# A two-layer decoder trunk: the residual stream turned from features on partitions to tokens on partitions

## The chip, the cores and the metric

One core of one Trainium2 chip runs the whole program. The metric is the device time of one execution in microseconds (us); the kernel before takes 875.04 us, the median of 3 runs (874.21 to 877.12).

## The reference

For each of two layers, on 256 tokens of 1024 features in float32 (cut to what matters):

```python
h = rmsnorm(x, norm_mix[i]);  z = h @ w_in[i]            # 1024 -> 5400 columns
y_a = nsa_mixer(...) @ w_up_nsa[i];  y_b = retention(...) @ w_up_ret[i]
mix = sigmoid(merge_a) * y_a + sigmoid(merge_b) * y_b
x = x + mix @ w_out[i]                                   # "out"
h = rmsnorm(x, norm_mlp[i])
x = x + square(relu(h @ w_ff1[i])) @ w_ff2[i]            # "ff1", "ff2": 1024 -> 4096 -> 1024
gate = sigmoid(rmsnorm(x, norm_ple[i]) @ w_ple_gate[i])  # "gate"
x = x + gate * (p[i] @ w_ple[i])                         # "ple"
```

`rmsnorm(x, g)` is x times the root r of 1/(mean of x squared + 1e-6), per token, times a gain per feature.

## The kernel before, in words

Every product is made of three TensorE matmuls in a 32-bit format of less precision: each operand is split in a high part (ScalarE copies it, `act`) and a low part (VectorE subtracts, `sub`), and `three` adds high x high, high x low and low x high in PSUM. The weights come from memory in units of 128 x 1024 floats (512 KB). For each unit SyncE issues a load into one of 4 `raw` buffers (line 310), ScalarE writes `hi` and VectorE writes `lo` (`unit_split`, lines 314 to 325), 6 buffers each, up to 4 units ahead of the one in use (`advance`, `take`). `PLAN` is the order of the units; the TensorE order is written out by hand (`ORDER`, and the body of `layer`), while the order of ScalarE, VectorE and GpSimd is left to the framework, which goes by readiness and priority. Generators for the attention work are put between the matmuls by a model of time (`poke`, `charge`).

The residual stream lies in `XT`, a tile of 128 x 8 x 256: feature within its chunk of 128 on the partitions, chunk, token. A norm stage (`new_stage`) holds `XH` and `XL`, the high and low parts of x times the gain, in the same layout; there are three stages in a layer (mixer, MLP, gate), and the factor r is brought in after the product. `feed_x` makes one chunk of `XH` (ScalarE, 256 columns) and of `XL` (VectorE, 256 columns). `feed_sq` squares two chunks (ScalarE) and adds the squares up, on VectorE or, for chunks 2 to 5, on GpSimd (`gp`, line 209). `finish_a` sums the squares over the partitions with matmuls against a column of ones (4 TensorE instructions `pt<-ones,z`) and makes r by a power on GpSimd; `finish_b` spreads r over the partitions with two TensorE transposes (`pt<-cst,r`, line 220) and a ScalarE copy to `RB`.

Two ways of multiplying stand in the kernel. In `b_unit`, `wide` and the loops of ple and gate the 128 x 128 weight block is stationary and 256 tokens stream past it: 24 matmuls of 256 columns for a unit. In `a_unit` (used for q, rv, rg and others of the first product) 128 x 128 of the activations are stationary and 512 weight columns stream: 12 matmuls of 512 columns for a unit.

The tail of a layer runs thus. `out` has 8 units; four accumulators, one for each two chunks of features, two in the PSUM tag `sc` and two in `pt`, take `wide` products (`out_k`). The last two units are used together for one accumulator after the other, and behind each accumulator VectorE adds it to `XT` and `feed` makes the stage of the MLP. `ff1` (16 pairs of units, PSUM tag `mm`) and `ff2` (32 units, the same four accumulators) then take turns. At the end of ff2 each accumulator is multiplied by `RB` (`dz`), added to `XT` and fed. `ple` has 2 units; its result `pw` waits in SBUF. `gate` has 8 units in four groups of two chunks; `gate_tail` multiplies by `RB`, takes tanh, multiplies with `pw`, adds to `XT`, and feeds the next layer's stage or, in the last layer, sends the chunks out. The next layer starts with the units kcvc, kvg and q, all from the fed stage.

Of the kernel before, what the change touches and what calls it, by code (L numbers as in the profile page):

```python
# [15 lines left out]
P = 128  # L16
# [29 lines left out]
for _n, _w in PAR_PARTS:  # L46
# [8 lines left out]

ORDER = (
# [7 lines left out]
def _seq(s):  # L64
    return [(x, 0) if x in ("fa", "fb") else (x[:-1], int(x[-1])) for x in s.split()]
# [5 lines left out]
def _plan(l):  # L71
    r = [({"w": "w1"}.get(n, n), u) for n, u in SEQ[l] if n not in ("fa", "fb")]
# [10 lines left out]
    r += [("gate", u) for u in (0, 2, 4, 1, 3, 5, 6, 7)]  # L83
    return [(l,) + x for x in r]
# [11 lines left out]
def trunk(ctx: ExitStack, tc: tile.TileContext, xT, wu, wg, cst, msk, par, pin, out):  # L96
# [131 lines left out]

    XT = bp.tile([P, 8, S], F32, tag="S0", name="XT")
    PR = [cp.tile([P, NHEAD], F32, tag=f"par{l}", name=f"par{l}") for l in range(DEPTH)]  # L230
# [44 lines left out]
    def load_early(k):  # L275
# [113 lines left out]
    def new_stage(l, which):  # L389
# [7 lines left out]
            "sq": None,  # L397
        }

    def feed_x(st, c0, n):  # L400
        t0 = cur[0]
        for c in range(c0, c0 + n):
            fresh(t0)
            g = st["g"][:, c:c + 1]
            act(st["XH"][:, c, :], XT[:, c, :], AF.Copy, scale=g)
            stt(out=st["XL"][:, c, :], in0=XT[:, c, :], scalar=g,
# [19 lines left out]
    def feed(st, c0, n=2):  # L426
        feed_x(st, c0, n)
        feed_sq(st, c0, n)

    def finish_a(st):  # L430
        sq = st["sq"]
        pr = p_tile([P, 2])
        for t in range(2):
            mm(pr[:, t:t + 1], sq[:, 0, t * P:(t + 1) * P], ones, start=True, stop=True)
        ms = small([P, 2], "ms")
        ts(out=ms, in0=pr, scalar1=1.0 / D, scalar2=EPS, op0=ALU.mult, op1=ALU.add)
# [4 lines left out]
    def finish_b(st, square=False):  # L441
# [5 lines left out]
        if square:  # L447
            act(RB, pb.rearrange("p a b -> p (a b)"), AF.Square)
        else:
            act(RB, pb.rearrange("p a b -> p (a b)"), AF.Copy)  # L450
# [43 lines left out]
    def layer(l, st):  # L494
# [392 lines left out]
        for name, u in SEQ[l]:  # L887
            if name == "kcvc":
                b_unit(pkv, take(l, "kcvc", u), XH, XL, 4 * u, u == 0, u == 1)
                if u == 1:  # L890
                    ready("kcvc")
            elif name == "fa":
# [98 lines left out]
        def accumulators():  # L991
            return [(s_tile, p_tile)[n % 2]([P, 2, S]) for n in range(4)]

        po = []

        def out_k(k):
# [3 lines left out]
            for n in range(4):  # L1000
                wide(po[n], w, n, MH[:, k, :], ML[:, k, :], k == 0, False)
# [21 lines left out]
        for n in range(4):  # L1023
            wide(po[n], w6, n, MH[:, 6, :], ML[:, 6, :], False, False)
            wide(po[n], w7, n, MH[:, 7, :], ML[:, 7, :], False, True)
            xc = XT[:, 2 * n:2 * n + 2, :]
            tt(out=xc, in0=xc, in1=po[n], op=ALU.add)
            feed(stf, 2 * n)
# [14 lines left out]
        def ff1(i):  # L1043
            pm = mm_tile([P, 2, S])
            for u in range(2):
                b_unit(pm, take(l, "ff1", 2 * i + u), XH, XL, 4 * u, u == 0, u == 1)
# [12 lines left out]
        def ff2(i):  # L1059
            h, o = ff.pop(i)  # L1060
            for u in range(2):
# [3 lines left out]
                for n in range(4):  # L1065
                    wide(pf[n], w, n, h[:, u, :], o[:, u, :], i == 0 and u == 0, False)

        ff1(0)
        finish_a(stf)
        ff1(1)  # L1070
        finish_b(stf, square=True)
        for i in range(14):
            ff1(i + 2)
# [4 lines left out]
        dz = [big([P, 2, 2, S], f"B{1 + i}", "dz") for i in range(2)]  # L1078
        h, o = ff.pop(15)
        for n in range(4):  # L1080
            for u in range(2):
                wide(pf[n], ws[u], n, h[:, u, :], o[:, u, :], False, u == 1)
            d = dz[n // 2][:, n % 2]
            tt(out=d, in0=pf[n], in1=bc2(stf["RB"]), op=ALU.mult)
            xc = XT[:, 2 * n:2 * n + 2, :]
            tt(out=xc, in0=xc, in1=d, op=ALU.add)
            feed(stp, 2 * n)


        pw = big([P, 8, S], "S5", "pw")  # L1090
        for u in range(2):
            wh, wl = take(l, "ple", u)
            vh = wh.rearrange("p (k n) -> p k n", k=2)
            vl = wl.rearrange("p (k n) -> p k n", k=2)
            for n in range(2):
                pm = mm_tile([P, 2, S])
                for k in range(2):
                    for q in range(2):
                        c = (2 * n + q) * P
                        three(pm[:, q, :], vh[:, k, c:c + P], vl[:, k, c:c + P], ph[:, k, :],  # L1100
                              pl[:, k, :], k == 0 and q == 0, k == 1 and q == 1)
                c = 4 * u + 2 * n
                with tc.high_priority():
                    act(pw[:, c:c + 2, :], pm, AF.Copy, scale=0.5)
# [4 lines left out]
        Z = [big([P, 4, S], f"B{3 * i}", "gz") for i in range(2)]  # L1109

        def gate_tail(pm, c0, n):
            z = Z[c0 // 4][:, c0 % 4:c0 % 4 + n, :]
            tt(out=z, in0=pm, in1=stp["RB"].unsqueeze(1).to_broadcast([P, n, S]), op=ALU.mult)
            act(z, z, AF.Tanh, scale=0.5)
            stt(out=z, in0=z, scalar=1.0, in1=pw[:, c0:c0 + n, :], op0=ALU.add, op1=ALU.mult)
            xc = XT[:, c0:c0 + n, :]
            tt(out=xc, in0=xc, in1=z, op=ALU.add)
            if stn is not None:
                feed(stn, c0, n)
            else:  # L1120
                nc.sync.dma_start(out[:, c0:c0 + n, :], xc)

        pms = [mm_tile([P, 2, S]) for _ in range(3)]
        for u in range(2):
            for j in range(3):
                b_unit(pms[j], take(l, "gate", 2 * j + u), XH, XL, 4 * u, u == 0, u == 1)
                if u == 1 and j == 0:
                    finish_a(stp)
                if u == 1 and j == 1:
                    finish_b(stp)  # L1130
                    gate_tail(pms[0], 0, 2)
                    gate_tail(pms[1], 2, 2)
        gate_tail(pms[2], 4, 2)
        ws = [take(l, "gate", 6 + u) for u in range(2)]
        for n in range(2):
            pm = s_tile([P, 1, S])
            for u in range(2):
                vh = ws[u][0].rearrange("p (k n) -> p k n", k=4)
# [143 lines left out]
```

## Time and profile before

| | |
|---|---|
| median of 3 runs | 875.04 us (874.21 to 877.12) |
| profiled execution | 876.97 us, of which the span from first to last instruction is 875.1 us |
| TensorE busy | 851.6 us, 97% of the span, 6649 matmuls |
| VectorE busy | 613.2 us (70%) |
| ScalarE busy | 502.6 us (57%) |
| GpSimd busy | 59.1 us (7%) |
| DMA | 152.11 MB, 174 GB/s on average |
| mean granted TensorE clock | 0.989 of full speed |

The busy time of TensorE counts a matmul from its start to its modelled end, which overlaps the next matmul; so how fast matmuls follow one another is read from their starts, or from the chain of work that ended last, which counts each piece only up to the next. In the profile, L215 is the matmul helper, L220 the transpose helper, L184 a ScalarE activation, L188 a VectorE two-tensor operation, L196 a VectorE scalar-tensor-tensor operation and L209 a GpSimd two-tensor operation. A tile is named with its operands, as `mm<-XH,hi`: written to `mm` from the moving `XH` and the stationary `hi`.

### The profile page before, as it was taken

To read this page: it belongs to the slowest core of one execution; us is meant where nothing else is said; L and a number is where in the kernel's file an instruction comes from. 1 tells how busy PE (TensorE), PEld (TensorE's weight loads), DVE (VectorE), ACT (ScalarE), POOL (GpSimd) and SP (SyncE) were. 2 spreads that over 40 slices of the span, in tenths; PEclk is the share of its full clock that TensorE was granted. 3 is DMA by queue.
4 is the path that set the end of the run, shared out by engine and by line. 5 is a ranking of instruction groups with operands and counts; after the bars stand their busy time and mean duration, and the time that the engine had idled before them with its cause. 6 is when DMAs were issued, how large, how long until landed. Compare 5 with 4: busy or idle time off the path is not lost.

```text
span 875.1 us, 16496 instructions
## 1 busy us (share of the span) xinstructions
PE 851.6 (97%) x6649; PEld 822.9 (94%) x6649; DVE 613.2 (70%) x997; ACT 502.6 (57%) x838; POOL 59.1 (7%) x44
## 2 busy tenths in 40 slices
PE   7989999989999999999999999999899999999997
PEld 6888899989999999999987988999899999999997
DVE  5988797866865555556898888887668555555585
ACT  6776786544654444445676878775347444444461
POOL 2120000000200000000222100000003000000020
PEclk8999999989999999999999999999999999999999
DMA  7857544436476656656655563543455666656541
GB/s 232 315 185 231 167 126 140 127 104 191 127 235 185 181 189 188 179 189 203 220 160 169 183 205 118 169 125 119 147 181 170 194 187 189 178 189 189 179 139 49
DMA packets 43852, 152.11 MB, mean 174 GB/s; under 512 B 5120, under 2 KB 6144, under 8 KB 43776
## 3 DMA queue, kind: packets, MB, share of 16 engines
q1 hardware_dynamic: 43776, 151.06, 55.8%
q8 instruction: 52, 0.85, 0.4%
q14 instruction: 24, 0.20, 0.1%
HBM read 149.99 MB, written 1.05 MB: 173 GB/s over the span
## 4 chain that ended last, share of the span: by engine, by line
PE 85%; DVE 8%; issue 2%; POOL 2%; DMA 1%; ACT 1%; SPq 0%; DVEq 0%; ACTq 0%; POOLq 0%
PE mm L215 51%; PE sc L215 16%; PE pt L215 14%; PE ot L215 3%; DVE lo L188 3%; PE pt L220 2%; POOL rso L209 1%; DMA raw<-in_wu_dram 1%; DVE zt L188 1%; DVE XL L196 1%; DVE zs L188 0%; ACT tmp L184 0%; DVE gz L196 0%; DVE XT L188 0%; ACT hi L184 0%
## 5 line engine op out<-in xcount | busy, mean ns | idle before, releaser
L188 DVE TENSOR_TENSOR lo<-raw,hi 128x1024 fp32r<-128x1024 f32 (+2 forms) x285 | 341.1, 1204 | 184.4 <-ACT hi L184 183.5
L184 ACT ACTIVATE hi<-raw 128x1024 fp32r<-128x1024 f32 (+2 forms) x285 | 295.5, 1045 | 280.1 <-PE mm L215 156.6
L215 PE MATMUL mm<-XH,hi 128*128 128x256 f32 x992 | 283.4, 286 | 0.0
L215 PE MATMUL mm<-XH,lo 128*128 128x256 f32 x992 | 279.3, 282 | 0.0
L215 PE MATMUL mm<-XL,hi 128*128 128x256 f32 x992 | 279.1, 281 | 0.0
L215 PEld LDWEIGHTS mm<-XH,hi 128*128 128x128 f32 x992 | 186.8, 188 | 1.1
L215 PEld LDWEIGHTS mm<-XL,hi 128*128 128x128 f32 x992 | 186.9, 188 | 0.8
L215 PEld LDWEIGHTS mm<-XH,lo 128*128 128x128 f32 x992 | 186.8, 188 | 0.0
L215 PE MATMUL pt<-ho,hi 128*128 128x256 f32 x512 | 96.6, 281 | 0.0
L215 PE MATMUL sc<-ho,hi 128*128 128x256 f32 x512 | 96.6, 281 | 0.0
L215 PEld LDWEIGHTS pt<-ho,hi 128*128 128x128 f32 x512 | 78.6, 188 | 0.0
L215 PEld LDWEIGHTS sc<-ho,hi 128*128 128x128 f32 x512 | 78.5, 188 | 0.0
L215 PE MATMUL sc<-ho,lo 128*128 128x256 f32 x256 | 72.0, 281 | 0.0
L215 PE MATMUL pt<-ho,lo 128*128 128x256 f32 x256 | 72.0, 281 | 0.0
L215 PE MATMUL mm<-hi,XH 128*128 128x512 f32 (+2 forms) x160 | 57.6, 360 | 0.0
L215 PE MATMUL mm<-hi,XL 128*128 128x512 f32 (+2 forms) x160 | 56.4, 352 | 0.0
L215 PE MATMUL mm<-lo,XH 128*128 128x512 f32 (+2 forms) x160 | 56.3, 352 | 0.0
L215 PEld LDWEIGHTS sc<-ho,lo 128*128 128x128 f32 x256 | 48.2, 188 | 0.0
L215 PEld LDWEIGHTS pt<-ho,lo 128*128 128x128 f32 x256 | 48.2, 188 | 0.0
L184 ACT ACTIVATE e<-e,nmx 128x128 f32<-128x128 f32 (+2 forms) x96 | 37.7, 395 | 11.9 <-DVE nmx L204 11.8
L209 POOL TENSOR_TENSOR rso<-rsv,mhalf 128x2 f32<-128x2 f32 (+3 forms) x18 | 23.8, 1324 | 295.8 <-DVE rsv L192 287.1
L209 POOL TENSOR_TENSOR z<-z,z 128x512 f32<-128x512 f32 x12 | 20.3, 1692 | 296.9 <-ACT pw L184 173.5
(181 smaller groups left out, 1345.0 us busy)
## 6 DMA issues: line engine op xcount, KB each, us to landing
raw<-in_wu_dram SPq DMA_DIRECT2D x275, 512.0 KB, 3.7
raw<-in_wg_dram SPq DMA_DIRECT2D x8, 280.0 KB, 3.2
XT<-in_xT_dram SPq DMA_DIRECT2D x3, 256.0 KB, 6.9
cst<-in_cst_dram SPq DMA_DIRECT2D x1, 768.0 KB, 7.9
out_dram<-XT SPq DMA_DIRECT2D x3, 256.0 KB, 2.4
raw<-in_wu_dram SPq DMA_DIRECT2D x2, 256.0 KB, 3.9
tmp<-in_pin_dram SPq DMA_DIRECT2D x2, 256.0 KB, 4.1
cmp<-in_par_dram SPq DMA_DIRECT2D x2, 144.0 KB, 4.4
```

What stands on the lines that cost most here:

```text
L184: return nc.scalar.activation(o, *a, **k)
L188: return nc.vector.tensor_tensor(**k)
L196: return nc.vector.scalar_tensor_tensor(**k)
L209: return nc.gpsimd.tensor_tensor(**k)
L215: return nc.tensor.matmul(o, a, b_, **k)
L220: return nc.tensor.transpose(o, a, i)
```

## The change

The stream is kept as `X`, 128 tokens on the partitions x 2 token halves x 1024 features. It is loaded from a second copy of the input (`xk`, 1 MB, issued on SyncE's queue behind the 40th weight unit) into the SBUF place of `XT`, which is only used for the first stage. In out, ff2, ple and gate the activations are now stationary and 512 weight columns stream (`wide`, `a_unit`); the four accumulators are quarters (token half, feature half) in the order (0,0), (1,0), (0,1), (1,1). With tokens on the partitions r is a factor per partition: ff2 adds its result with r squared in one VectorE operation, gate takes r in the scale of tanh, and `dz`, `RB` and `finish_b` go from those two stages. The squares are summed along the row by ScalarE (`square`, with an accumulator), so that `finish_a` needs no matmul and no GpSimd addition. For the stage of the next product `turn_x` turns half of the features: 8 TensorE transposes of 128 x 128 into two PSUM tiles, from which ScalarE and VectorE make `XH` and `XL`. The first half is turned behind the third quarter, the second half behind the first unit that uses the first half (at ff1, whose first four units are reordered), between the two ple units, or at `tr` in the next layer's order. The first layer's first stage is fed as before.

```diff
+    "kcvc0 kvg0 tr kvg1 kcvc1 fa kvg2 kvg3 fb q0 q1 q2 q3 w0 w1 ksvs0 ksvs1 w2 w3 w4 rq0 rq1 w5  "
...
-    r += [("ff1", u) for u in range(4)]
+    r += [("ff1", u) for u in (0, 2, 1, 3)]
...
+        if k == 40:
+            X.append(bp.tile([P, 2, D], F32, tag="S0", name="X"))
+            nc.sync.dma_start(X[0], xk)
...
+    def turn_x(st, n, tiles):
+        for j in range(2):
+            c0 = 4 * n + 2 * j
+            pt = tiles[j]([P, 2, S])
+            for c in range(2):
+                for t in range(2):
+                    flip(pt[:, c, t * P:(t + 1) * P], X[0][:, t, (c0 + c) * P:(c0 + c + 1) * P], ident)
+            feed_x(st, c0, pt)
+
+    def square(st, t, n):
+        if st["ss"] is None:
+            st["ss"] = small([P, 2, 2], "ssx")
+        act(ztile([P, 512]), xs(t, n), AF.Square, accum_out=st["ss"][:, t, n:n + 1])
...
-    def wide(o, w, n, ah, al, f, z):
-        for q in range(2):
-            c = (2 * n + q) * P
-            three(o[:, q, :], w[0][:, c:c + P], w[1][:, c:c + P], ah, al,
-                  f and q == 0, z and q == 1)
+    def wide(o, w, t, n, ah, al, f, z):
+        a, b = t * P, n * 512
+        three(o, ah[:, a:a + P], al[:, a:a + P], w[0][:, b:b + 512], w[1][:, b:b + 512], f, z)
...
+        for i, (t, n) in enumerate(quads):
+            wide(po[i], w6, t, n, MH[:, 6, :], ML[:, 6, :], False, False)
+            wide(po[i], w7, t, n, MH[:, 7, :], ML[:, 7, :], False, True)
+            fresh()
+            tt(out=xs(t, n), in0=xs(t, n), in1=po[i], op=ALU.add)
+            if i == 2:
+                turn_x(stf, 0, (mm_tile, mm_tile))
...
+        ff1_unit(0, 0)
+        turn_x(stf, 1, (s_tile, p_tile))
+        ff1_unit(1, 0)
+        for t, n in quads:
+            square(stf, t, n)
+        ff1_unit(0, 1)
+        ff1_unit(1, 1)
         finish_a(stf)
-        ff1(1)
-        finish_b(stf, square=True)
+        r2 = small([P, 2], "r2")
+        tt(out=r2, in0=stf["r"], in1=stf["r"], op=ALU.mult)
...
+            stt(out=xs(t, n), in0=pf[i], scalar=r2[:, t:t + 1], in1=xs(t, n), op0=ALU.mult, op1=ALU.add)
+            if i == 2:
+                turn_x(stp, 0, (mm_tile, mm_tile))
...
+        for n in range(2):
+            w = take(l, "ple", n)
+            pms = [mm_tile([P, 512]) for _ in range(2)]
+            a_unit(pms, w, ph, pl, 0, 2, 512, True, True)
...
+            if n == 0:
+                turn_x(stp, 1, (s_tile, p_tile))
+                for t, m in quads:
+                    square(stp, t, m)
+                finish_a(stp)
...
+        def gate_tail(pm, t, n):
+            fresh()
+            z = Z[n][:, t, :]
+            act(z, pm, AF.Tanh, scale=rg[:, t:t + 1])
+            stt(out=z, in0=z, scalar=1.0, in1=pw[:, t, n * 512:(n + 1) * 512], op0=ALU.add, op1=ALU.mult)
+            tt(out=xs(t, n), in0=xs(t, n), in1=z, op=ALU.add)
+            if stn is not None:
+                square(stn, t, n)
+            else:
+                nc.sync.dma_start(out[:, t, n * 512:(n + 1) * 512], xs(t, n))
...
+            if n == 1 and stn is not None:
+                turn_x(stn, 0, (s_tile, s_tile))
+            ws = [take(l, "gate", 4 * n + u) for u in (2, 3)]
+            for t in range(2):
...
+                gate_tail(pms[t], t, n)
```

## Rows read from the trace of the kernel before

**Rows 1.** The page: span, and busy time by engine (share, instructions).
```profile
span 875.1 us, 16496 instructions
PE 851.6 (97%) x6649; PEld 822.9 (94%) x6649; DVE 613.2 (70%) x997; ACT 502.6 (57%) x838; POOL 59.1 (7%) x44
```
**Rows 2.** The page: the chain that ended last, share by engine.
```profile
PE 85%; DVE 8%; issue 2%; POOL 2%; DMA 1%; ACT 1%; SPq 0%; DVEq 0%; ACTq 0%; POOLq 0%
```
**Rows 3.** The chain in time, first ff1 units: start us, us, what.
```profile
230.41 5.69 PE mm L215 x48
236.10 0.44 PE pt L215 x4
236.54 5.80 PE mm L215 x48
242.34 0.34 PE pt L220 x2
```
**Rows 4.** The 512-column matmuls: their group by form, then the chain.
```profile
L215 PE MATMUL mm<-lo,XH 128*128 128x512 f32 x96 | 37.8, 394 | 0.0
...
88.40 4.20 PE mm L215 x18
...
522.73 4.18 PE mm L215 x18
```
**Rows 5.** The chain, transposes between attention matmuls in layer 1.
```profile
544.68 0.44 PE pt L220 x4
545.12 0.71 PE mm L215 x6
```
**Rows 6.** The chain, gate of layer 1 to the end.
```profile
858.56 0.34 PE pt L215 x4
...
861.86 0.22 PE pt L220 x2
...
864.93 5.71 PE sc L215 x48
...
872.03 0.42 DVE XT L188
```
**Rows 7.** TensorE's timeline, start of layer 1; in brackets idle before, and releaser.
```profile
445.75 0.39 PE L215 MATMUL ot<-XL,hi 128*128 128x256 f32 x1 [0.46 <-DVE XL L196]
...
452.88 0.58 PE L215 MATMUL pt<-ones,z 128*128 128x1 f32 x4 [0.33 <-DVE z L188]
...
456.89 0.43 PE L220 MATMUL pt<-cst,r 128*128 128x128 f32 x2 [0.25 <-POOL r L209]
```
**Rows 8.** Stretches: length, busy PE, PEld, DVE, ACT, POOL; clock, DMA share, GB/s.
```profile
246.00:407.00 161.00, 161.00 (x1360) 161.00 (x1359) 88.37 (x87) 75.58 (x85) 0.95 (x1) 1.00 0.62 188
443.00:490.00 47.00, 43.27 (x286) 38.48 (x285) 41.55 (x75) 33.91 (x59) 13.64 (x9) 1.00 0.54 168
616.90:620.30 3.40, 3.40 (x16) 3.40 (x17) 0.98 (x1) 0.00 (x0) 0.00 (x0) 0.50 0.37 82
```
**Rows 9.** Timelines of VectorE, ScalarE and GpSimd: start us, us, operation.
```profile
408.88 1.23 DVE L188 TENSOR_TENSOR lo<-raw,hi 128x1024 fp32r<-128x1024 f32 x1 [1.62 <-ACT hi L184]
442.75 3.74 DVE L196 SCALAR_TENSOR_TENSOR XL<-XT,par,XH 128x256 fp32r<-128x256 f32 x4
471.99 0.88 DVE L196 SCALAR_TENSOR_TENSOR KT<-pt,gk,KT 128x256 fp32r<-128x256 f32 x2
...
407.79 1.06 ACT L184 ACTIVATE hi<-raw 128x1024 fp32r<-128x1024 f32 x1 [1.79 <-PE pt L215]
471.03 0.47 ACT L184 ACTIVATE KT<-pt,gk 128x256 fp32r<-128x256 f32 x1
...
442.70 2.71 POOL L209 TENSOR_TENSOR z<-z,z 128x512 f32<-128x512 f32 x2 [10.73 <-ACT z L184]
```
**Rows 10.** DMA issues of the result: KB each, median us to landing.
```profile
out_dram<-XT SPq DMA_DIRECT2D x3, 256.0 KB, 2.4
out_dram<-XT SPq DMA_DIRECT2D x2, 128.0 KB, 1.8
```

More of the change, by code (lines that the diff above doesn't have):

```diff
@@ L64, in _seq @@
 def _seq(s):
-    return [(x, 0) if x in ("fa", "fb") else (x[:-1], int(x[-1])) for x in s.split()]
+    return [(x, 0) if x in ("fa", "fb", "tr") else (x[:-1], int(x[-1])) for x in s.split()]
 SEQ = [_seq(s) for s in ORDER]
 def _plan(l):
-    r = [({"w": "w1"}.get(n, n), u) for n, u in SEQ[l] if n not in ("fa", "fb")]
+    r = [({"w": "w1"}.get(n, n), u) for n, u in SEQ[l] if n not in ("fa", "fb", "tr")]
     for n in ("ma", "mb"):
@@ L82, in _plan @@
     r += [("ple", u) for u in range(2)]
-    r += [("gate", u) for u in (0, 2, 4, 1, 3, 5, 6, 7)]
+    r += [("gate", u) for u in range(8)]
     return [(l,) + x for x in r]
@@ L424, in feed_sq, with xs @@
             tt(out=acc[:, 0], in0=acc[:, 0], in1=acc[:, 1], op=ALU.add)
-    def feed(st, c0, n=2):
-        feed_x(st, c0, n)
-        feed_sq(st, c0, n)
+    def xs(t, n):
+        return X[0][:, t, n * 512:(n + 1) * 512]
+    def turn_x(st, n, tiles):
[10 more added lines that the diff above has]
+        act(ztile([P, 512]), xs(t, n), AF.Square, accum_out=st["ss"][:, t, n:n + 1])
     def finish_a(st):
[L431 to L434, printed above, removed]
         ms = small([P, 2], "ms")
+        if st["ss"] is None:
+            pr = p_tile([P, 2])
+            for t in range(2):
+                mm(pr[:, t:t + 1], st["sq"][:, 0, t * P:(t + 1) * P], ones, start=True, stop=True)
+        else:
+            pr = small([P, 2], "ssum")
+            tt(out=pr, in0=st["ss"][:, :, 0], in1=st["ss"][:, :, 1], op=ALU.add)
         ts(out=ms, in0=pr, scalar1=1.0 / D, scalar2=EPS, op0=ALU.mult, op1=ALU.add)
@@ L439, in finish_a, with finish_b @@
         st["r"] = r
-    def finish_b(st, square=False):
+    def finish_b(st):
         r = st["r"]
@@ L891, in layer @@
                     ready("kcvc")
+            elif name == "tr":
+                turn_x(st, 1, (p_tile, p_tile))
             elif name == "fa":
@@ L1041, in layer, with ff1_unit, ff1_end @@
         sub(pl, pT, ph.bitcast(F32))
[L1043 to L1046, printed above, removed]
+        def ff1_unit(i, u):
+            if u == 0:
+                ff[i] = mm_tile([P, 2, S])
+            b_unit(ff[i], take(l, "ff1", 2 * i + u), XH, XL, 4 * u, u == 0, u == 1)
+            if u == 1:
+                ff1_end(i, ff[i])
+        def ff1_end(i, pm):
+            fresh()
             au = big([P, 2, 2, S], f"B{i % 3}", "au")
@@ L1077, in layer @@
         ws = [take(l, "ff2", 30 + u) for u in range(2)]
-        dz = [big([P, 2, 2, S], f"B{1 + i}", "dz") for i in range(2)]
         h, o = ff.pop(15)
-        for n in range(4):
+        for i, (t, n) in enumerate(quads):
             for u in range(2):
[L1082 to L1087, printed above, removed]
@@ L1090, in layer @@
[L1090 to L1104, printed above, removed]
+                wide(pf[i], ws[u], t, n, h[:, u, :], o[:, u, :], False, u == 1)
@@ new lines, in layer @@
+            fresh()
+            stt(out=xs(t, n), in0=pf[i], scalar=r2[:, t:t + 1], in1=xs(t, n), op0=ALU.mult, op1=ALU.add)
+            if i == 2:
+                turn_x(stp, 0, (mm_tile, mm_tile))
+        pw = big([P, 2, D], "S5", "pw")
+        for n in range(2):
+            w = take(l, "ple", n)
+            pms = [mm_tile([P, 512]) for _ in range(2)]
+            a_unit(pms, w, ph, pl, 0, 2, 512, True, True)
+            with tc.high_priority():
+                for t in range(2):
+                    act(pw[:, t, n * 512:(n + 1) * 512], pms[t], AF.Copy, scale=0.5)
+            if n == 0:
[3 more added lines that the diff above has]
+                finish_a(stp)
+                rg = small([P, 2], "rg")
+                ts(out=rg, in0=stp["r"], scalar1=0.5, scalar2=None, op0=ALU.mult)
@@ L1106, in layer @@
         stn = new_stage(l + 1, 0) if l + 1 < DEPTH else None
         XH, XL = stp["XH"], stp["XL"]
[L1109 to L1117, printed above, removed]
+        def gate_tail(pm, t, n):
+            fresh()
+            z = Z[n][:, t, :]
+            act(z, pm, AF.Tanh, scale=rg[:, t:t + 1])
+            stt(out=z, in0=z, scalar=1.0, in1=pw[:, t, n * 512:(n + 1) * 512], op0=ALU.add, op1=ALU.mult)
+            tt(out=xs(t, n), in0=xs(t, n), in1=z, op=ALU.add)
@@ L1118, in gate_tail @@
             if stn is not None:
-                feed(stn, c0, n)
+                square(stn, t, n)
             else:
[L1121 to L1132, printed above, removed]
```

73 lines of the change are left out of this document (34 added, 39 removed), and 1 row of the table ORDER.

## Prediction

> **What bounds the kernel now.** I read the page first, then the chain that ended last as shares and in order of time, then stretches and timelines. TensorE is busy for 97% of the span [rows 1] and holds 85% of the chain [rows 2]. Between the layers' beginnings there is no gap at all: from 246 to 407 us TensorE is busy for 161.00 of 161.00 us, while VectorE has 88, ScalarE 76 and DMA a share of 0.62 [rows 8]. So in out, ff1, ff2, ple and gate time is the number of matmuls times their spacing, and a VectorE or ScalarE instruction saved there is worth nothing by itself. Only where a stage's input is late does TensorE wait: from 443 to 490 us, the start of layer 1, it is busy for 43.27 of 47.00 us [rows 8].
>
> **Matmuls.** The spacing of 256-column matmuls is 5.69 us / 48 = 118.6 ns [rows 3]. Two pay 237.2 ns. The kernel already has 512-column matmuls of the new kind (moving weights, stationary activations): 18 of them take 4.20 and 4.18 us, 233.3 and 232.2 ns each [rows 4]; I take the mean, 232.7. A pair turned into one saves 4.5 ns (3.9 to 5.0 by the two rows). The units concerned are 8 of out, 32 of ff2, 2 of ple and 8 of gate, 50 in a layer and 100 in all, each with 24 matmuls before and 12 after: 1200 x 4.5 ns = **5.4 us less** (4.7 to 6.0). Only 2% is won, since the streaming of columns, which stays, is nearly all of it.
>
> The Trainium skill (TensorE: Matmul & The Clock Gate, Back-to-back issue gap) gives an isolated matmul N/2.4 + 2.5 ns, so that a pair made one would save the 2.5 ns alone, an estimate of 3.0 us for 1200. These rows show another slope and a dearer start, and by that rule the sum would be 2.4 us higher.
>
> **Transposes added.** `turn_x` runs at five stages (MLP and gate of both layers, the mixer of layer 1), twice each: 10 x 8 transposes. Four transposes between matmuls take 0.44 us of the chain [rows 5], 0.11 each, so 80 cost **8.8 us more**. They stand in TensorE's own order, where nothing hides them.
>
> **TensorE work removed.** `finish_a` loses its four `ones` matmuls at five of six stages: at the MLP stage 0.44 us and 0.11 more in the next 48 matmuls (5.80 against 5.69) [rows 3], at the gate stage 0.34 [rows 6]. I take 0.5 each, **2.5 us less** (1.7 to 2.8). `finish_b` goes at four: 0.34 us at each MLP stage [rows 3] and 0.22 at each gate stage [rows 6], **1.1 us less**. So far TensorE's own work is 0.2 us longer: transposes eat what the matmuls win.
>
> **Waits at the start of layer 1.** Three waits stand there: 0.46 us for `XL`, 0.33 for the squares, 0.25 for r [rows 7]. A matmul is shown as longer than its spacing (394 against 233 ns [rows 4]), so each of these hides about 0.16 us more: 1.5 us together. They have one cause: after the last gate matmul VectorE has to multiply by `RB`, do two more operations and make `XL`, and four of those take 3.74 us beside a GpSimd addition of the squares [rows 9]; an `XL`-like operation out of PSUM without one takes 0.44 (0.88 for two). After the change the first half is turned and fed during the second half of gate; kcvc0 and kvg0 then need nothing that is late, and neither the squares nor GpSimd's additions stand before TensorE. **1.5 us less**, in a range from 0.5 to 1.8, since the second half could be late in its turn (below).
>
> **What each new wait costs.** At out and ff2 the first transposes wait for the second quarter's addition, with the third quarter's matmuls (6 x 233 ns = 1.4 us) as cover; the addition takes 0.69 (VectorE's 256 columns take 0.42 [rows 6] and its 1024 columns 1.23 [rows 9], so 512 lie a third of the way). Then at out 8 transposes (0.88) and the fourth quarter (1.4) cover the feed: the first two chunks are there after 0.44, then 0.47 for `XH` and 0.44 for `XL` [rows 9], so 1.35 us against 2.28, and each further chunk takes less on either engine than the 0.71 us that ff1 spends on one (6 matmuls, as in [rows 5]). What could get in between are the `hi` and `lo` of weight units, 1.06 and 1.23 us, but ScalarE waits for TensorE to free a buffer before each one [rows 9]: all six are full, and as the last two units are held until the fourth quarter ends, hardly one can start in that stretch. At ff2 the ple units stand between, so there is more cover. Behind a late transpose stand the fourth quarter and all of ff1; behind them in turn nothing but the split units, which have four units of lead.
>
> At `tr` the last quarter's tail is tanh, a product and a sum, 0.67 + 0.69 + 0.69 us (ScalarE's 512 columns again a third of the way, from 0.47 to 1.06 [rows 9]), against kcvc0 and kvg0, 24 x 119 ns and 12 of 280 columns at about 129 ns, 4.4 us; kvg1 then covers the feed of chunk 4. Both `hi` buffers come free just then, so one split on each engine may stand ahead, 2.3 us more, and just fit. I put 0.5 us on all new waits together (0 to 7, see the rivals). `square` costs ScalarE about what it costs now, and r is wanted only at the end of ff2 and in tanh. The load of `X`, 1 MB on SyncE's queue, delays the units behind it by about two loads; they run units ahead, at a DMA share that even in the densest stretch is 0.62 [rows 8]. I take nothing (0 to 1).
>
> **The end.** Now 0.42 us operations on 256 columns follow each other, four of them, and 128 KB leave in 1.8 us [rows 6, 10]. Afterwards three on 512 columns, about 2.0 us against 1.8, and 256 KB in 2.4 us [rows 10]: **0.8 us more**.
>
> **Sum.** -5.4 + 8.8 - 2.5 - 1.1 - 1.5 + 0.5 + 0.8 = -0.4 us. The profiled execution took 876.97 us, 1.9 over its span of 875.1 [rows 1], so it would become 876.6; it lies 1.9 us above the median of 875.04, and from the median I forecast **874.6 us**, with 872 to 877 as this case's own range.
>
> **Rivals.**
> (a) *The feed is late (slower).* The place is VectorE between the transposes and the first ff1 unit and at `tr`. If two `lo` stand ahead of the first `XL` at out, it comes 2.5 us later, 1.5 after TensorE wants it; with half a microsecond for an addition behind a `lo`, 2 us at each of two outs, 0.5 at each ff2, and 2 at `tr`: 7 us, so 881. It decides from about 3 us of such waits on. For it: VectorE is the busier of the two, and nothing can be fed now until three quarters are done, where before chunks were fed after each. Against it: the full buffers.
> (b) *More of the start of layer 1 goes (faster).* The idle time there is 3.7 us [rows 8]; VectorE, at 41.55 of 47.00 us, is what the chain runs over there, and it loses the `RB` products, the additions of squares and the slow `XL`s. If the later waits go as well, that is another 2 us; and the stretch at 616.90 with the clock at the lower of its two levels (0.50 for 3.40 us [rows 8]) costs up to 1.7, and may fall elsewhere once everything before it shifts. Together 874.6 - 3.7, so 871. Against it: layer 0 has later waits of the same kind without that backlog, as q's norm is a chain over three engines.
> (c) *The change doesn't do what it says (slower).* If 512 columns of ff2 cost two times 118.6 ns after all, as its stationary blocks come fresh from `ho`, the 5.4 us are not there: 880.
> (d) *The clock.* The trace has transposes in fours [rows 5], and over the stretch from 443 to 490 us, in which those of k and q fall, the clock stays at 1.00 [rows 8]. If eight in a row counted as idleness and each group brought a half-clock stretch as at 616.90, that is 10 x 1.7 us: 891. The Trainium skill (TensorE: Matmul & The Clock Gate, Part 4: PE-mode transpose) says that transposes don't count as activity in the same way; this would speak against the change, but matmuls stand on either side of every group.
>
> **How the numbers follow.** Forecast 0.56, (a) 0.15, (b) 0.19, (c) 0.06, (d) 0.04. About 0.3%, 2.6 us, is what can be told from no change. The forecast gives 0.12 faster, 0.42 same, 0.02 slower; (a) 0.02 same and 0.13 slower; (b) 0.18 faster, 0.01 same; (c) and (d) 0.09 slower and 0.01 same. Faster 0.30, same 0.46, slower 0.24. The range reaches from (b) with the upper bound of the matmuls, 870, to (a) at 881, and leaves out (d) and the worst of (a).
>
> **What would show it.** 12 matmuls of an ff2 unit in 2.79 us; 8 transposes in 0.88 us; no wait before the first ff1 unit or `tr` over half a microsecond; layer 1's first three waits gone; 2 us from the last matmul to the last DMA issue. The forecast is wrong if the spacing at 512 columns is not 232 to 234, or if transposes wait.

## The result and the profile after

The kernel after takes **881.53 us** (median of 4 runs, 881.27 to 883.05); the kernel before took 875.11 beside it. The ratio is 1.0074, with an interval of 1.0053 to 1.0095: slower by 4.6 to 8.3 us. The forecast was 874.6, in a range from 870 to 881. The profiled execution took 881.68 us and its span is 879.2, 4.0 more than the span of before [rows 1]. The page of the kernel after: span and busy time by engine.

```profile
span 879.2 us, 14188 instructions
PE 851.0 (97%) x5501; PEld 769.1 (87%) x5501; DVE 594.5 (68%) x973; ACT 503.9 (57%) x851; POOL 33.8 (4%) x34
```

TensorE does what was computed for it: 1148 matmuls fewer, 0.6 us less busy time. GpSimd is relieved by 25 us and VectorE by 19, and nothing came of that. The loss lies in TensorE's idle time, its clock and its spacing in ff1, and it shows when the span is cut where TensorE starts a stage. The starts are read from TensorE's timeline; the columns give the length of each stage, the difference, and what the terms of the sum give for that stage (all of them except the 0.5 us for new waits).

| stage | before | after | difference | forecast |
|---|---|---|---|---|
| start to the retention's up product, layer 0 | 187.04 | 186.36 | -0.7 | 0 |
| from there through out to ff1, layer 0 | 43.21 | 42.60 | -0.6 | +0.45 |
| ff1 to the start of layer 1 | 212.30 | 213.78 | +1.5 | -0.3 |
| start of layer 1 to the first use of `ZB` | 27.19 | 27.59 | +0.4 | -1.1 |
| from there to q's last transposes | 17.85 | 21.30 | +3.45 | 0 |
| from there to the retention's up product | 128.43 | 128.14 | -0.3 | 0 |
| from there through out to ff1, layer 1 | 42.16 | 41.01 | -1.15 | +0.45 |
| ff1 to the last matmul | 212.17 | 212.76 | +0.6 | -1.2 |
| last matmul to the end | 4.79 | 5.64 | +0.85 | +0.8 |

How the forecast is spread: 8 transposes (0.88) stand in out, 32 in layer 0's stage from ff1 on (3.5), 8 at the start of layer 1 and 24 in the last product stage; 42 of a layer's 50 units with the new kind of matmul lie behind ff1 (42 x 12 x 4.5 ns = 2.27 us). Two stages are shorter than forecast by over a microsecond, both times because less of a half-clock stretch (granted clock 0.50) lies in them: before has such stretches from 186.8 to 193.6 and from 616.9 to 620.3 us, after from 188.0 to 191.5 and from 485.0 to 488.4. What they cost is seen in the kernels of the experiments, where the same stage of layer 1 takes 41.0 us with no such stretch in it (a tile for each chunk), 42.5 with 3.4 us of it (all three edits) and 43.8 with 6.8 us (the feed raised). The last one moved from out to q, so a part of q's +3.45 belongs to out's -1.15. The first row holds the load of `X`, for which the sum had nothing; no loss shows, though after also has 3.4 us less at half clock before 20 us, which could hide up to 1.7.

**Right by the rows.** The chain that ended last, in the kernel after: start us, us, what; first matmuls in the MLP of layer 1, then eight transposes for the input of gate.

```profile
680.16 0.69 PE sc L216 x3
...
685.74 5.76 PE mm L216 x48
...
842.91 0.87 PE mm L221 x8
```

The 24 matmuls of 512 columns of an ff2 pair take 5.58 us (680.16 to 685.74), 232.5 ns each, and eight transposes 0.87, as computed. What was not foreseen stands between: 48 matmuls of ff1, which the change does not touch, take 5.76 us instead of 5.69 [rows 3], 120.0 ns each instead of 118.6.

**A wait inside the third ff1 unit** (the first to use the second half of the features). TensorE's timeline of the kernel after, layer 0: ff1's first matmul, and the wait; the bracket is the idle time before and its releaser.

```profile
228.96 0.28 PE L216 MATMUL mm<-XH,hi 128*128 128x256 f32 x1
...
237.74 0.28 PE L216 MATMUL mm<-XH,hi 128*128 128x256 f32 x1
238.84 0.39 PE L216 MATMUL mm<-XL,hi 128*128 128x256 f32 x1 [0.83 <-DVE XL L197]
```

From start to start 1.10 us lie between the last two instead of 0.12: 0.98 us lost, and 0.94 at the same place in layer 1. It stands in front of the unit's fourth and last chunk. ScalarE and VectorE in that stretch:

```profile
229.91 2.02 ACT L185 ACTIVATE hi<-raw 128x1024 fp32r<-128x1024 f32 x2
...
232.42 1.07 ACT L185 ACTIVATE hi<-raw 128x1024 fp32r<-128x1024 f32 x1
...
235.18 0.48 ACT L185 ACTIVATE XH<-sc,par 128x256 fp32r<-128x256 f32 x1 [0.96 <-DVE XL L197]
235.68 1.06 ACT L185 ACTIVATE hi<-raw 128x1024 fp32r<-128x1024 f32 x1
236.65 0.46 ACT L185 ACTIVATE XH<-pt,par 128x256 fp32r<-128x256 f32 x1
...
231.20 3.55 DVE L189 TENSOR_TENSOR lo<-raw,hi 128x1024 fp32r<-128x1024 f32 x3
234.66 0.48 DVE L197 SCALAR_TENSOR_TENSOR XL<-sc,par,XH 128x256 fp32r<-128x256 f32 x1
...
235.69 0.48 DVE L197 SCALAR_TENSOR_TENSOR XL<-sc,par,XH 128x256 fp32r<-128x256 f32 x1
...
237.06 0.16 DVE L189 TENSOR_TENSOR r<-r 128x2 f32<-128x2 f32 x1 [0.81 <-POOL r L210]
237.17 1.23 DVE L189 TENSOR_TENSOR lo<-raw,hi 128x1024 fp32r<-128x1024 f32 x1
238.31 0.48 DVE L197 SCALAR_TENSOR_TENSOR XL<-pt,par,XH 128x256 fp32r<-128x256 f32 x1
```

The second half lies in two PSUM tiles, `sc` and `pt`, with two chunks in each. The second `XH` from `sc` reads nothing that VectorE writes, and yet it waits 0.96 us for the first `XL` from `sc`: the two engines take turns on a tile. That first `XL` is itself late, behind three `lo`. In the pause that the turn makes a split gets its place on either engine (`hi` at 235.68, `lo` at 237.17), and VectorE also stands idle for 0.81 us at `r`, a part of the norm's factor, until GpSimd has taken its power. So the fourth `XL` comes 2.6 us after the third, where in a row it would come after 0.4. The Trainium skill (PSUM — Partial Sum Buffer, PSUM bank collisions raise a hardware error) says that two engines must not touch one 2 KiB bank at once, reads against reads included; a tile of 2 x 256 floats on a partition fills just such a bank, and the trace agrees in that `XH` starts at 235.18, right when the first `XL` on its tile is over. No run here shows what would happen without the turns.

**Two waits at the start of layer 1.** TensorE's and VectorE's timelines of the kernel after.

```profile
450.65 0.39 PE L216 MATMUL ot<-XL,hi 128*128 128x256 f32 x1 [0.81 <-DVE XL L197]
452.57 0.38 PE L216 MATMUL ot<-XL,hi 128*128 128x256 f32 x1 [0.91 <-DVE XL L197]
...
447.85 2.35 DVE L189 TENSOR_TENSOR lo<-raw,hi 128x1024 fp32r<-128x1024 f32 x2
450.12 0.87 DVE L197 SCALAR_TENSOR_TENSOR XL<-pt,par,XH 128x256 fp32r<-128x256 f32 x2
450.90 1.22 DVE L189 TENSOR_TENSOR lo<-raw,hi 128x1024 fp32r<-128x1024 f32 x1
452.04 0.87 DVE L197 SCALAR_TENSOR_TENSOR XL<-pt,par,XH 128x256 fp32r<-128x256 f32 x2
```

The waits of before are gone from here (`XL` at 445.75, the squares at 452.88, r at 456.89 [rows 7]), but two new ones came, 0.97 and 1.10 us from start to start: two `lo` ahead of the first pair of `XL`, and a third `lo` between the pairs, in the pause in which ScalarE has its turn on the tiles.

**The wait in q.** VectorE, GpSimd and TensorE of the kernel before.

```profile
472.78 1.27 DVE L200 TENSOR_REDUCE qss<-tmp 128x8 f32<-128x512 f32 x2
...
477.64 2.54 POOL L209 TENSOR_TENSOR rso<-rsv,mhalf 128x8 f32<-128x8 f32 x1 [0.89 <-DVE rsv L192]
...
482.79 0.63 PE L220 MATMUL pt<-cst,qn 128*128 128x128 f32 x4 [0.86 <-DVE qn L188]
```

ScalarE, VectorE, GpSimd and TensorE of the kernel after.

```profile
472.94 0.62 ACT L185 ACTIVATE tmp<-tmp 128x512 f32<-128x512 f32 x1
...
476.77 0.69 DVE L189 TENSOR_TENSOR tmp<-tmp,rso 128x512 f32<-128x512 f32 x1 [1.53 <-POOL rso L210]
477.38 0.68 DVE L201 TENSOR_REDUCE qss<-tmp 128x8 f32<-128x512 f32 x1
...
479.96 2.54 POOL L210 TENSOR_TENSOR rso<-rsv,mhalf 128x8 f32<-128x8 f32 x1 [3.22 <-DVE rsv L193]
...
485.48 0.90 PE L221 MATMUL pt<-cst,qn 128*128 128x128 f32 x3 [3.10 <-DVE qn L189]
```

q's second half is to be divided by its norm, whose power GpSimd takes. In the kernel before VectorE sums both halves' squares in a row (`qss` twice, from 472.78), and GpSimd's second power starts at 477.64, 0.89 us behind the first. Now ScalarE has the second squares ready at 473.56 (`tmp<-tmp`), but the second `qss` stands behind an instruction that itself waits for GpSimd's first power, so GpSimd stands idle for 3.22 us, and TensorE for 3.10; from start to start the wait is 3.27 us, against 1.02 before. Towards its end, at 485.0 us, the half-clock stretch begins. Stretches of the kernel after (length, busy PE, PEld, DVE, ACT, POOL; clock, DMA share, GB/s), the first of which answers to that of before [rows 8]:

```profile
443.00:490.00 47.00, 40.83 (x258) 36.27 (x256) 36.29 (x67) 31.11 (x54) 10.30 (x7) 0.96 0.48 157
485.00:488.40 3.40, 2.92 (x14) 2.92 (x15) 2.81 (x8) 3.18 (x4) 1.91 (x2) 0.50 0.50 159
```

TensorE is idle for 6.2 us in the first stretch, against 3.7 before, although VectorE has 5.3 us less to do in it.

**The end.** The last two VectorE operations of the kernel after, where before three operations of VectorE and one of ScalarE took 0.42 us each [rows 6].

```profile
874.70 0.69 DVE L197 SCALAR_TENSOR_TENSOR gz<-gz,pw 128x512 f32<-128x512 f32 x1 [1.38 <-ACT gz L185]
875.42 0.69 DVE L189 TENSOR_TENSOR X<-X,gz 128x512 f32<-128x512 f32 x1
```

The result leaves in four issues of 256 KB, 2.2 us to landing (median), as against five [rows 10].

### The profile page after: what moved, and what is told of

It reads as the page before. It is cut to its first block, busy times and chain, and to the rows that moved or that the text cites. A ratio compares the mean times of both kernels' runs of the same rounds, so it can differ in the third digit from the quotient of the medians.

```text
span 879.2 us, 14188 instructions
## 1 busy us (share of the span) xinstructions
PE 851.0 (97%) x5501; PEld 769.1 (87%) x5501; DVE 594.5 (68%) x973; ACT 503.9 (57%) x851; POOL 33.8 (4%) x34
## 5 line engine op out<-in xcount | busy, mean ns | idle before, releaser
L216 PE MATMUL mm<-XL,hi 128*128 128x256 f32 x896 | 252.8, 282 | 1.6 <-DVE XL L197 1.6
L216 PE MATMUL sc<-hi,ho 128*128 128x512 f32 x256 | 100.6, 396 | 0.0
L216 PE MATMUL pt<-hi,ho 128*128 128x512 f32 x256 | 100.5, 395 | 0.0
L216 PEld LDWEIGHTS pt<-hi,ho 128*128 128x128 f32 x256 | 48.2, 188 | 11.3
L216 PEld LDWEIGHTS sc<-hi,ho 128*128 128x128 f32 x256 | 48.2, 188 | 9.9
L216 PE MATMUL sc<-lo,ho 128*128 128x512 f32 x128 | 50.6, 396 | 0.0
L216 PE MATMUL pt<-lo,ho 128*128 128x512 f32 x128 | 50.3, 393 | 0.0
L216 PEld LDWEIGHTS mm<-hi,XL 128*128 128x128 f32 x224 | 42.2, 188 | 7.0
L216 PEld LDWEIGHTS mm<-hi,XH 128*128 128x128 f32 x224 | 42.2, 188 | 5.9
L216 PEld LDWEIGHTS mm<-lo,XH 128*128 128x128 f32 x224 | 42.2, 188 | 5.9
```

The lines of the kernel that those rows point to most:

```text
L216: return nc.tensor.matmul(o, a, b_, **k)
```

## Experiments

The times are medians; each group was timed beside the kernel before on the same chip.

### Is the new kind of matmul worth anything?

```diff
+    def halves(o, ah, al, bh, bl, f, z):
+        for q in range(2):
+            d = 256 * q
+            three(o[:, d:d + 256], ah, al, bh[:, d:d + 256], bl[:, d:d + 256], f and q == 0, z and q == 1)
...
-        three(o, ah[:, a:a + P], al[:, a:a + P], w[0][:, b:b + 512], w[1][:, b:b + 512], f, z)
+        halves(o, ah[:, a:a + P], al[:, a:a + P], w[0][:, b:b + 512], w[1][:, b:b + 512], f, z)   # likewise in ple and gate
```

> The changed kernel, but each 512-column matmul of out, ff2, ple and gate is issued as two of 256 columns with the same stationary block: only the matmul width is undone. Theory Q (the loss lies in VectorE and ScalarE work that stands in a worse order ahead of the norm inputs, and the wider matmuls bring what the trace of before promised): 1200 pairs of 118.6 ns against 1200 of 232.7, so about 5.4 us above the changed kernel, or 3.7 if the ff1 matmuls, which went from 118.7 to 120.0 ns apart in the changed kernel, fall back to 118.7. Rival W (512 columns win nothing in these stages): no difference from the changed kernel. The waits at ff1 and at the start of layer 1 stay by both.

885.1 us (882.81 to 887.53), 3.6 more than the kernel after. The four runs lie in two pairs 4.5 us apart, so the medians alone say little, and the reading goes by the stages. Twelve of the split matmuls take 1.42 us in the chain, 118.6 ns each, against 232.5 for one of 512. The chain in the MLP of layer 1 of this kernel:

```profile
680.33 0.71 PE pt L216 x6
681.04 0.71 PE sc L216 x6
...
685.32 5.69 PE mm L216 x48
```

The ff1 row at 5.69 hides a part of the price: the spacing of 120.0 ns is gone here, so the 3.6 us stand against a kernel that pays up to 1.8 us for it. In the stages behind ff1 this kernel is slower by 1.1 (214.92 against 213.78) and 1.2 us (213.94 against 212.76); with 0.8 to 1.0 us for ff1, and 0.35 for its wait, which is 0.60 us in the first unit here instead of 0.94 to 0.98 in the third, that is 2.3 to 2.5 each, and the sum had 2.27. Rival (c) falls.

### What do the transposes cost, and what the feed behind them?

Both kernels make `XH` and `XL` from `X` as it lies, with tokens on the partitions, so the products behind them are of other numbers; the work is the same. The first leaves the transposes out, the second makes all 80 and does not read them.

```diff
-            pt = tiles[j]([P, 2, S])               # kept in the second kernel
-            for c in range(2):                     # kept in the second kernel
-                for t in range(2):                 # kept in the second kernel
-                    flip(pt[:, c, ...], X[0][:, t, ...], ident)
-            feed_x(st, c0, pt)
+            feed_x(st, c0, X[0][:, :, c0 * P:(c0 + 2) * P])
```

> The changed kernel without its 80 transposes: XH and XL are made straight from X in SBUF, in X's own layout, so the products are of other numbers. Theory Q: 80 x 0.11 = 8.8 us of TensorE go and the waits behind the feed (about 1 us at the third ff1 unit of each layer, 2.1 at the first units of layer 1) go too, as the feed can start 0.5 to 0.9 us sooner: 8.8 + 2 to 4, so 869 to 871; the 3.3 us wait for the second half of q stays. Rival P (ScalarE and VectorE, which take turns on one PSUM tile of transposes, are what makes the feed late): the same here. Rival W says nothing here. If the transposes were hidden: no change.

> The changed kernel with its 80 transposes, but nothing reads them: XH and XL are made from X in SBUF, in X's own layout, so the products are of other numbers. It parts TensorE's time for the transposes from the feed out of PSUM. Theory Q (order of the queues): the feed is ready sooner by the transposes alone, and waits that come from a split unit standing ahead of XL stay: within 1.5 us of the changed kernel, 880 to 882. Rival P (turn-taking on a PSUM tile): the waits at ff1 go in both layers and most of those at the start of layer 1, so 4 us less, 877 to 878.

Without transposes 867.23 us (866.24 to 869.99), with 80 unread ones 876.96 (874.37 to 879.11), with the real ones 881.53. So the transposes themselves cost 9.7 us by the medians and 7.3 by the profiled spans (867.9 and 875.2); the forecast was 8.8. The cleanest measure is the stage from layer 1's ff1 to the last matmul, without a half-clock stretch and with ff1 at 118.7 ns in both kernels: 210.61 against 207.93 us, 0.11 for each of its 24 transposes. Reading them costs another 4.6 us: rival P's 877 to 878 came, not theory Q's 880 to 882, and the kernel without transposes is some 2 us faster than was expected. In both kernels no wait is left in ff1 and none at the start of layer 1, while the wait in q stays at 3.27 us. The second kernel is level with before (ratio 1.0017, 0.9997 to 1.0037). That the feed is what waits is shown by this. Why it waits is not: from `X` the feed is free of the tiles, and also of the transposes' place in TensorE's order.

### Rank or tile?

The feed raised in rank; and, in a second kernel, a PSUM tile for each chunk of the second half instead of one for two.

```diff
-            feed_x(st, c0, pt)
+            with tc.high_priority():
+                feed_x(st, c0, pt)
```

> Only the rank of the feed from the PSUM tiles is raised (norm inputs put ahead of what the scheduler would otherwise set before them on ScalarE and VectorE). Theory T (two engines take turns on a PSUM tile that holds two chunks, so the fourth XL comes after four steps): the waits before the third ff1 unit (0.99 and 0.94 us) and at layer 1's start (0.97 and 1.1 us) stay within 0.3 us each; 881 to 882. Theory S (the weight splits that stand ahead of XL on VectorE make it late): the two waits at ff1 fall under 0.4 us, together at least 1 us; 880 or less. In either the 3.3 us wait in q of layer 1 stays.

```diff
-        for j in range(2):
-            c0 = 4 * n + 2 * j
-            pt = tiles[j]([P, 2, S])
-            for c in range(2):
+        m = len(tiles)
+        for j in range(m):
+            k = 4 // m
+            c0 = 4 * n + k * j
+            pt = tiles[j]([P, k, S])
+            for c in range(k):
...
-        turn_x(stf, 1, (s_tile, p_tile))           # likewise at the gate and at tr
+        turn_x(stf, 1, (s_tile, p_tile, s_tile, p_tile))
```

> The second half of the norm input is turned into four PSUM tiles, one for each chunk, instead of two tiles of two chunks. Theory T (turns on a tile): with a tile for each chunk ScalarE and VectorE work on different tiles at once; both waits at ff1 (0.99, 0.94) and the second of the two at layer 1's start (1.1) fall under 0.4 us, about 2 to 3 us in all: 878.5 to 879.5. Theory S (splits ahead of XL): they stay, 881 to 882. The 3.3 us wait in q stays in both. Rival N (four tiles ask more of the PSUM ring, so a transpose waits for a tile): waits of over 0.3 us ahead of transposes appear and eat the gain, 881 or more.

Rank: 881.28 us, nothing won. The waits stay (0.93 in layer 0's ff1, 0.98 and 1.11, 0.93), but so does VectorE's order, `lo` three times ahead of the first `XL` in ff1 and twice at the start of layer 1; the scheduler put the splits there all the same. So this run only shows that rank does not help; it does not speak against the splits.

A tile for each chunk: **875.81 us** (872.52 to 877.87), ratio to before 0.9999 (0.9981 to 1.0017). TensorE's first matmul of ff1, VectorE in ff1 and at the start of layer 1, and TensorE's one remaining wait there:

```profile
230.33 0.28 PE L216 MATMUL mm<-XH,hi 128*128 128x256 f32 x1
...
232.57 2.36 DVE L189 TENSOR_TENSOR lo<-raw,hi 128x1024 fp32r<-128x1024 f32 x2
234.84 0.48 DVE L197 SCALAR_TENSOR_TENSOR XL<-sc,par,XH 128x256 fp32r<-128x256 f32 x1
235.24 0.48 DVE L197 SCALAR_TENSOR_TENSOR XL<-pt,par,XH 128x256 fp32r<-128x256 f32 x1
235.63 0.48 DVE L197 SCALAR_TENSOR_TENSOR XL<-sc,par,XH 128x256 fp32r<-128x256 f32 x1
236.02 0.48 DVE L197 SCALAR_TENSOR_TENSOR XL<-pt,par,XH 128x256 fp32r<-128x256 f32 x1
...
449.46 0.87 DVE L197 SCALAR_TENSOR_TENSOR XL<-pt,par,XH 128x256 fp32r<-128x256 f32 x2
450.25 0.87 DVE L197 SCALAR_TENSOR_TENSOR XL<-sc,par,XH 128x256 fp32r<-128x256 f32 x2
...
450.00 0.39 PE L216 MATMUL ot<-XL,hi 128*128 128x256 f32 x1 [0.82 <-DVE XL L197]
```

The waits in ff1 are gone in both layers, but two things changed there at once. Counted from ff1's first matmul, the first `XL` comes after 4.51 us, where in the kernel after it came after 5.70, since two `lo` stand ahead of it and not three; and the fourth follows the first after 1.18 us instead of 3.65, as the four now stand in a row. TensorE lacked 0.98 us, so either would have covered it. The kernel with 256-column halves parts the two. VectorE and ScalarE of that kernel:

```profile
233.07 0.48 DVE L197 SCALAR_TENSOR_TENSOR XL<-sc,par,XH 128x256 fp32r<-128x256 f32 x1
...
234.90 0.48 DVE L197 SCALAR_TENSOR_TENSOR XL<-pt,par,XH 128x256 fp32r<-128x256 f32 x1
...
233.58 0.48 ACT L185 ACTIVATE XH<-sc,par 128x256 fp32r<-128x256 f32 x1 [0.96 <-DVE XL L197]
```

The turn is there, with the same 0.96 us, and the first `XL` comes no sooner than in the kernel after (5.89 us behind ff1's first matmul at 227.18). But no split lies between the first and the fourth, which follows after 1.83 us, and it ends 8.20 us behind ff1's first matmul, where TensorE of the kernel after wanted it at 8.90: the third unit does not wait. So a turn by itself makes no wait in ff1. What made it is the work let in at the turn, behind a first `XL` that was late already.

At the start of layer 1 the first pair of `XL` stands 7.38 us behind the layer's first matmul in both kernels, with the two `lo` ahead of it, and the wait for it stays at 0.98 us. The second pair follows after 0.79 us instead of 1.92, and the wait of 1.10 us is gone. So theory T holds as it stands for that one wait, theory S, by the timeline, for the one that stays, and the two waits in ff1 needed, by these times, both the late first `XL` and the work let in at the turn. The edit as a whole takes three waits away (0.98 + 0.94 + 1.10 = 3.0 us); no transpose waits for a tile, so rival N falls. The whole gain of 5.7 us is more than the 2 to 3 expected. ff1's spacing is back at 118.7 ns in both layers, worth about 1.8, which no theory had in it; the rest is within the spread of the runs.

### The sums of q

Layer 1's squares and sums of q are raised in rank.

```diff
-            sq = tmp([P, NH, DH])
-            act(sq, zc, AF.Square)
-            ss = small([P, NH], "qss")
-            reduce_sum(ss, sq)
+            with tc.high_priority() if l else ExitStack():
+                sq = tmp([P, NH, DH])
+                act(sq, zc, AF.Square)
+                ss = small([P, NH], "qss")
+                reduce_sum(ss, sq)
```

> The changed kernel, but in layer 1 the squares and the sum of q's second token half get a higher priority, so that VectorE makes that sum before it waits for GpSimd's power of the first half, as the kernel before has it. Nothing else changes. Theory Q: the wait of TensorE before the second half's transposes falls from 3.3 us to about 1.0, as in the kernel before, and the 3.4 us at half clock behind it, worth up to 1.7, are not entered: 2.3 to 4.0 us less than the changed kernel, about 878. If that wait only takes the place of another one: no change.

878.33 us (874.37 to 880.15), 3.2 less than the kernel after. VectorE, GpSimd and TensorE of this kernel:

```profile
475.92 0.68 DVE L201 TENSOR_REDUCE qss<-tmp 128x8 f32<-128x512 f32 x1
...
478.39 2.54 POOL L210 TENSOR_TENSOR rso<-rsv,mhalf 128x8 f32<-128x8 f32 x1 [0.89 <-DVE rsv L193]
...
483.44 0.66 PE L221 MATMUL pt<-cst,qn 128*128 128x128 f32 x4 [0.82 <-DVE qn L189]
```

The second sum is ahead of the waiting instruction, GpSimd's second power follows the first after 0.89 us as in the kernel before, the 3.27 us wait is back at 0.98, and the half-clock stretch behind it is gone: the stage takes 17.16 us instead of 21.30. The waits in ff1 and at the start of layer 1 are as in the kernel after.

### Both together

First a tile for each chunk, the feed raised and q's sums raised in layer 1; then the same with q's sums raised in both layers, together with the roots behind them.

> A tile for each chunk, the feed raised in rank, and layer 1's two sums of q's squares put early. If the feed's waits and the q wait are what the changed kernel lost, both gains add: 881.5 - 3.2 - (2 to 3) = 875.3 to 876.3, which is the kernel before within 0.3%, with the 256-column spacing at either 118.7 or 120.0 ns deciding another 1 to 2 us. If they lie on the same chain, no better than the better one of them, 878.

> As the kernel with both, but in both layers and with the reciprocal roots that follow q's sums put early too, so that GpSimd is asked for them sooner. If the wait behind q (0.98 us left with the sums early alone) is GpSimd's roots standing in line, it falls to under 0.5 us: 874.5 to 875.5. If it is the wait for TensorE's own place for the turned q, nothing changes against the kernel with both.

The kernel with all three edits takes **871.4 us** (870.71 to 872.73), ratio to before 0.9957 (0.9942 to 0.9971): the layout of the change, with two queues put right, is faster than both kernels. It is also 4 us better than its expectation, which did not reckon with the half-clock stretches: behind the first 20 us it has 3.4 us of them (611.0 to 614.4), where before has 10.2. They are not the whole of it: at the same mean granted clock of 0.993 its three executions have spans of 869.1 to 870.3 us, and three of the kernel before beside it 872.3 to 872.8. Its stages behind ff1 take 211.96 and 210.88 us, its stage of q 17.18. The other kernel, with the sums early in both layers and the powers with them, takes 872.3 (871.48 to 875.56); the waits behind q are the same (0.42 and 0.99 us). But the edit moved nothing there: VectorE's order in that stretch is the same, and GpSimd's first power starts 3.88 us behind the first use of `ZB` (470.21 and 466.33), 3.87 in the other (468.40 and 464.53). So this run does not tell whether GpSimd's powers are what is left; VectorE still stands idle for 0.92 us until the second one is there.

### The changed kernel once more

Nothing is altered.

> The changed kernel once more, nothing altered: is the 119.9 ns between ff1's 256-column matmuls its own, or a state of one execution? If it belongs to the kernel (Theory K), both layers show 119.9 again and the half-clock stretches are the same two (185 to 195 and 485 us). If it is a state of the execution (Theory E), as the near-identical kernel with the raised feed suggests with 118.7 in both layers, a layer or both show 118.7, and the span moves with it by 0.8 to 1.0 us a layer, and with the half-clock stretches by about 1.7 us for each 3.4 us. In either the waits at ff1 (0.99, 0.94), at layer 1's start (0.97, 1.1) and behind q (3.27) stand again to within 0.1 us, and the time is 879 to 883.

880.82 us (879.98 to 882.74), ratio 1.0063 (1.0045 to 1.0082). The waits stand again to 0.05 us (0.94 and 0.94, 0.97 and 1.10, 3.28). ff1 differs. The chain in layer 1:

```profile
685.52 5.70 PE mm L216 x48
```

TensorE's timeline for a stretch of layer 0:

```profile
268.73 0.28 PE L216 MATMUL mm<-XH,lo 128*128 128x256 f32 x1
...
270.53 0.28 PE L216 MATMUL mm<-XH,lo 128*128 128x256 f32 x1
```

The two starts lie 15 matmuls apart, 1.80 us or 120.0 ns for one, in layer 0; layer 1 runs at 118.7, where the first profile had 120.0. So it differs between executions of one kernel and between its layers, as theory E said, and is not a property of the kernel.

## Why the prediction failed

**What held.** The spacing at 512 columns (232.5 ns for 232.7), the transposes (0.87 us for eight), the `ones` matmuls and the transposes of r that went, and the end (+0.85 for +0.8). Where no wait is left and ff1 runs at its spacing of before, the terms add up: in the kernel with a tile for each chunk, layer 1 from ff1 to the last matmul takes 210.64 us, 1.5 less than before, where the sum had 1.2. So a forecast near zero for TensorE's own work was right, and rivals (c) and (d) were not: behind none of the ten new groups of transposes did the clock fall.

A slip of sign did no harm: the prediction calls TensorE's own work "0.2 us longer", while its four terms give 0.2 us less, and the sum goes by the terms.

**The step that failed is "What each new wait costs", with 0.5 us.** Measured are 0.98 and 0.94 us in ff1 and 2.25 us more in q, 4.2 us together, with a half-clock stretch behind the last; and with it failed the 1.5 us less at the start of layer 1. Three things were wrong.

*ff1.* The feed of the first half was worked out, with the fourth quarter as cover, and it did arrive in time. The second half was passed over with "each further chunk takes less on either engine than the 0.71 us that ff1 spends on one". That holds for each engine by itself (0.35 to 0.40 us from start to start), not for two engines that alternate on a tile, with three splits ahead and others let in at the change. "Hardly one can start in that stretch" holds up to the end of out; then buffers come free, and ScalarE starts three `hi` between 229.9 and 232.4, just ahead of the second half's feed.

*The start of layer 1.* "1.5 us less" became 0.3 more: two waits of 2.07 us together, for three of before and a fourth, small one, 1.76 us together, all from start to start. The old causes went as forecast, and the waits moved to the second half's `XL`. The text had this in "one split on each engine may stand ahead, 2.3 us more, and just fit"; VectorE had two ahead and a third in between.

*q.* No step and no rival saw a longer wait here; (b) named q's norm, but only as a wait that might go or stay. The change touches nothing in q; but the order of VectorE's queue is left to the framework, which goes by readiness and priority, and with the feed changed the second sum fell behind a waiting instruction. This one wait costs as much as the two in ff1 together, and with its half-clock stretch more (3.2 us by the run that put it right). What moved it there was not tried.

**Beside that step**: ff1's spacing, 0.8 to 1.0 us a layer, in both layers of the first profile of the kernel after and in layer 0 of the second. No term had it, and its cause stays open. Added up, the forecast's -0.4 with 3.7 us for the new waits, 1.8 for the start of layer 1, 1.8 for the spacing, -1.7 for 3.4 us less at half clock behind 20 us and -0.7 ahead of the up product gives 4.5 us, an estimate; the spans differ by 4.0.

**Rival (a)** had the sign, the time (881) and, loosely, two of three places, with 0.15; it put the MLP's wait ahead of the first ff1 unit, and it came in the third. Its mechanism was half right: splits stand ahead of the first `XL` at all four waits of the feed, and one, of 0.97 us, goes by them alone; the other three also need what was let in at the turns on a tile, which it did not know. The argument that kept it small, full buffers, was the wrong one to lean on. **Rival (b)** wanted the half-clock stretch at 616.90 to go, and it did, to q.

How much of the loss is the clock's can be bounded: taking only executions with a mean granted clock of 0.992, the kernel after has spans of 877.6 to 879.1 us (four executions) and the kernel before 873.0 to 876.0 (eleven). The medians, 878.2 and 874.7, lie 3.5 us apart, so some 3.5 of the 4.6 to 6.4 us are there at the same clock.

## What to carry to other kernels

When a product's input is turned through PSUM, count the two engines that read a tile as one: give each chunk a tile of its own, or the readers alternate and other queued work can slip in at a change of turn. After a change look at every in-order queue behind it, even in stages it does not touch: a short reduction that stands behind an instruction waiting for another engine can cost more than the edit's own terms. And a sum that cancels to nearly nothing (8.8 us added, 9.0 taken from TensorE) is decided by the waits, so these need the closest working, the second half of each transfer as much as the first.

## What was not expected of the hardware

- Matmuls of 256 columns with the same operands follow one another at 118.7 or at 120.0 ns (5.70 and 5.76 us for 48), steadily over many units, in either layer, and in one execution differently from another. It can change within a layer: in layer 1 of the kernel with all three edits the 120 matmuls of ff1 behind the turned second half take 14.40 us, 120.0 ns each, and later groups of 48 take 5.70. The waits do not decide it, as the kernel with the feed raised has them and 118.7 behind its first ff1 units. The cause is open.
- ScalarE waited 0.96 us for VectorE to finish reading the other half of a PSUM tile, although its own operation takes nothing from VectorE there. A tile for each half took this away.
- A half-clock stretch followed the 3.27 us wait in q in every profile with that wait, 3.4 us long in six and 6.8 in one (the feed raised), and none followed where the wait was 0.98.
